# First mixer: the values v made like the gates, from seven half-size products, with half of the weight sums added by transfers

## The chip, the cores and the metric

The kernel runs on one core of one Trainium2 chip. Its time is the device time of one launch in microseconds (us); the median of three runs is given. A profile is one execution recorded by the hardware profiler.

## The reference

The whole trunk has two layers, each a token mixer and a gated ConvFFN, with a LayerNorm after each. The change is in the first mixer, gated linear attention (GLA). Cut to what matters:

```python
def gla_mixer(x, w_in, w_gk2, b_gk, norm_w, w_out):      # x: 512 x 1024
    hk, hv = GLA_HEADS * GLA_DK, GLA_HEADS * GLA_DV      # 512, 1024
    proj = x @ w_in
    q, k, v, gate, gk_lr = jnp.split(proj, [hk, 2 * hk, 2 * hk + hv, 2 * hk + 2 * hv], axis=-1)
    gk = jax.nn.log_sigmoid((gk_lr @ w_gk2 + b_gk).astype(jnp.float32)) / GLA_NORMALIZER
    ...
    o = rms_norm(gla_chunked(qc, kc, vc, gc), norm_w)    # 4 heads, chunks of 64
    o = from_head_chunks(o).astype(x.dtype)
    return (o * jax.nn.silu(gate)) @ w_out
```

So v and the gates are both a product of x (512 x 1024) with a 1024 x 1024 part of w_in: v from column 1024, the gates from column 2048.

## The kernel before, in words

**Precision.** Every large product is made from three: a number is split into a high part in fp32r (ScalarE, a cast) and a low part (VectorE, the number less its high part), and high x high, high x low and low x high are summed in PSUM. `split_out` (line 714) is that pair of operations; its tiles are `wh` and `wl` for weights, `xh` and `xl` for x. `raw` is a loaded block of weights (128 x 1024 floats, 512 KB).

**Weights.** A plan lists the blocks of weights in the order of their use. SyncE loads them ahead into three `raw` buffers; a block is issued (cast and split) up to two or three blocks ahead of TensorE (`LOOKAHEAD`, `self.look`). Four pairs of `wh` and `wl` buffers exist, so a cast waits until TensorE is done with the block four before it; a load waits until the split of the block three before it in `raw`.

**The first mixer in stages.** (1) x is loaded, turned and split; q, k and the low-rank factor are made feature by feature (tiles `fm`). Beside them `prepare(hd)` makes the decays of head hd: a small product `z`, then exponentials on ScalarE and a scan and some ten products on VectorE (tiles `z`, `na`, `bc`, `e`). (2) v is made by `x_tm` (tiles `tm`): two halves of 512 columns, each 4 blocks of weights, each block against 4 groups of 128 tokens. A ScalarE copy takes each result out of PSUM (line 1518). Beside them `scores` makes the scores (`sa`) of two heads and `turn` their turned keys (`kt`). (3) The gates are made by `gated` (tiles `fold`, then `sg`), and beside them `core(hd)` runs the four heads: the products `ds` with v, the states on VectorE, the outputs `o`. `finish` multiplies the outputs with the gates. (4) The output product.

**Seven for eight.** `gated` cuts the 512 tokens, the 1024 inputs and the 1024 outputs in two each, which makes 8 products of quarter matrices; with sums of quarters of x (the forms `w1`, `v2`, `v3`, `v4`, made by `x_forms` on VectorE) and of w, 7 do (`GATED`: b11, b21, t1, t2, b22, t3, t4). Each of the 7 takes two blocks of weights (i = 0 and 2), each block against two groups of 128 tokens (r = 0, 1), with two chunks of inputs (j) in three terms: 2 x 2 x 2 x 3 = 24 matmuls of 128 x 512. They gather in four PSUM tiles, two for each of the two sides (`acc`). What a product adds to the results is taken out by `update`: by ScalarE copies, or by VectorE additions and subtractions of a PSUM tile and a kept tile (lines 1230, 1237, 1240). The sums of w are made on VectorE in `issue_gated`: t1 and t2 add a loaded block to the kept b11 block (`gw`, line 451), t3 subtracts and t4 adds (lines 454 and 456), two blocks each.

**The order of the work.** The program is one thread per engine. The main line pumps matmuls of the stage, and the smaller jobs (`prepare`, `scores`, `core`, `finish`) are tasks that are let in between by a modelled clock; a scheduler then fixes each engine's order. An engine takes its instructions strictly in that order, so an instruction that waits holds all behind it.

**Accumulating transfers** exist already in the ConvFFN's output product (lines 408 and 410): GpSimd issues a DMA that adds its source to a block in SBUF.

Of the kernel before, what the change touches and what calls it, by code (L numbers as in the profile page):

```python
# [12 lines left out]
AF = mybir.ActivationFunctionType  # L13
ALU = mybir.AluOpType

P = 128
# [16 lines left out]
GATED = (("b11", "a11", 0), ("b21", "a12", 1), ("t1", "w1", 1), ("t2", "v2", 0), ("b22", "v4", 1), ("t3", "v3", 0),  # L33
         ("t4", "a22", 0))
GATED_NEW = {"b11": "b11", "b21": "b21", "t1": "b12", "t2": "b22", "b22": "b22", "t3": "b11", "t4": "b21"}
LN_EPS = 1e-5
RMS_EPS = 1e-6
GLA_SCALE = 128.0 ** -0.5
# [30 lines left out]
def blk(i, n=P):  # L69
    return slice(i * n, i * n + n)  # L70


class Trunk:
# [339 lines left out]
    def issue_fold(self, group, name, quarter, i):  # L413
# [11 lines left out]
            self.fold_sum(*following[1:3], following[4])  # L425
        return [(wh[:, blk(j, S)], wl[:, blk(j, S)]) for j in range(n)]

    def gated_load(self, group, name, i):


        if name == "b11":
            t = self.mp.tile([P, 1024], F32, name=self.uid("gw"), tag="gw", bufs=2)
        else:
            t = self.rp.tile([P, 1024], F32, name=self.uid("raw"), tag="raw")
        quarter = GATED_NEW[name]
        col = group["col"] + (2 - int(quarter[2])) * S
        c0 = 2 * i + int(quarter[1]) - 1
        src = group["w"].rearrange("(c p) f -> p c f", p=P)[:, c0:c0 + 3:2, col:col + S]
        load = self.nc.sync.dma_start(t.rearrange("p (j f) -> p j f", j=2), src)
        if name == "b11":  # L440
            self.behind(load, self.load)
        group[name, i] = t

    def issue_gated(self, group, name, i):
        nc = self.nc
        t = group.pop((name, i))
        if name == "b11":
            group["sum", i] = t
        total = group["sum", i]
        if name in ("t1", "t2"):  # L450
            nc.vector.tensor_add(total, total, t)
            t = total
        elif name == "t3":
            nc.vector.tensor_sub(t, total, t)
        elif name == "t4":
            nc.vector.tensor_add(t, total, t)
            del group["sum", i]
        self.vec(1.24)
# [688 lines left out]
    def x_forms(self, forms):  # L1147


        nc = self.nc  # L1150
        pair = lambda t: t.rearrange("p (j i) -> p j i", j=2)

        def part(x, odd, tok, k):
            return x[:, 4 * k + odd:4 * k + odd + 3:2, tok:tok + 256]

        def full(odd, tok):
            ts = [self.slot("xq") for _ in range(2)]
            for k, t in enumerate(ts):
                self.behind(nc.vector.tensor_add(pair(t), *(part(x, odd, tok, k) for x in (self.xh, self.xl))),
                            self.split[1])  # L1160
            return ts

        def split(name, ts):
            forms[name] = []
            for t in ts:
                h, l = self.slot("xfh", F32R), self.slot("xfl", F32R)
                self.split_out(h, l, t)
                forms[name].append((h, l))
            self.set(("form", name), 2.0)

        def both(a, b, op, out):
            for x, y, o in zip(a, b, out):
                nc.vector.tensor_tensor(o, x, y, op)

        a = full(0, 256)
        yield 2.0
        b = full(1, 256)
        yield 2.0
        both(a, b, ALU.subtract, b)
        yield 3.0  # L1180
        split("w1", b)
        yield 3.0
        c = full(0, 0)
        yield 2.0
        both(c, a, ALU.subtract, a)
        yield 2.0
        both(b, c, ALU.subtract, b)
        yield 3.0
        split("v2", b)
        yield 3.0  # L1190
        c = full(1, 0)
        yield 2.0
        both(b, c, ALU.add, b)
        yield 3.0
        split("v4", b)
        b = c = None
        yield 4.0
        split("v3", a)

    def gated(self, sg, forms):  # L1200


        nc = self.nc
# [9 lines left out]
            return self.xh[:, chunk, tok:tok + P], self.xl[:, chunk, tok:tok + P]  # L1213

        def copied(ps):
            t = self.slot("sg")
            nc.scalar.copy(t, ps)
            return t

        def done(tb, hf, t, src):  # L1220
            nc.scalar.activation(t, src, AF.Silu)
            sg[tb][hf] = t
            self.set(("sg", tb, hf), 1.2)

        def update(name, r):
            p, x = acc[0][r], acc[1][r]
            if name == "b11":
                top[r] = copied(p)
            elif name == "b21":
                nc.vector.tensor_add(top[r], top[r], x)  # L1230
                done(r, 1, top[r], top[r])
            elif name == "t1":
                high[r] = copied(x)
            elif name == "t2":
                right[r] = copied(p)
            elif name == "b22":
                nc.vector.tensor_sub(right[r], x, right[r])
                done(r, 0, right[r], right[r])
            elif name == "t3":
                self.third = nc.vector.tensor_sub(high[r], high[r], p)  # L1240
                self.after = None, self.third
                done(2 + r, 0, high[r], high[r])
            elif name == "t4":
                done(2 + r, 1, self.slot("sg"), p)

        self.look = 3
        for name, form, at in GATED:
            if form[0] in "vw":
                self.wait(("form", form))
            for i in (0, 2):  # L1250
                if name == "t3" and i:
                    self.look = 2
                w = self.weight()
                if name == "t4":
                    self.after = ()
                for r in range(2):
# [9 lines left out]
            forms.pop(form, None)  # L1266
        self.look = LOOKAHEAD

    def gates(self, sg):
# [59 lines left out]
    def gla(self, li, g, b):  # L1329
# [10 lines left out]
        def lr_done(ps):  # L1340
# [75 lines left out]
        sg = [[None, None] for _ in range(NTB)]  # L1416
        y = [[None, None] for _ in range(NTB)]

        kts, turned = [None] * GH, []

        def turn(hd):
            pk = self.psum("kt")
# [4 lines left out]
        def scores(first):  # L1427
# [4 lines left out]
            for hd in pair:  # L1432
# [18 lines left out]
        def core(hd):  # L1451
# [59 lines left out]
            self.spawn(scores(hd))  # L1511
        for hd in range(GH):
            self.spawn(core(hd))
        forms = {}
        for hf in range(2):
            def v_done(tb, ps, hf=hf):
                v[tb][hf] = t = self.slot("v")
                nc.scalar.copy(t, ps)
                self.set(("v", tb, hf), 2.4)
# [538 lines left out]
```

## Time and profile before

| | |
|---|---|
| median of three runs | 1226.43 us (1226.0 to 1226.56) |
| the profiled execution | 1226.47 us |
| its span | 1224.8 us, so 1.7 us lie outside it |
| TensorE busy | 1218.5 us, 99% |
| VectorE, ScalarE, GpSimd busy | 897.4, 604.7, 145.5 us |
| moved by transfers | 146.25 MB, 119 GB/s over the span |

In the profile PE is TensorE, PEld its loading of the stationary operand, DVE VectorE, ACT ScalarE, POOL GpSimd, SP SyncE; a q behind a name is that engine's sequencer. A row of a group gives line, engine, operation, out<-in with shapes and count, then busy time and mean ns of one, then the idle time of the engine just before and what ended it. A row of a timeline gives start and duration in us. Stage (1) lasts to about 60 us, v from there to about 90, the gates to about 168.

### The profile page before, as it was taken

The numbers are of one execution on the slowest core, as the hardware profiler recorded it, in microseconds if no ns is written. First come the engines' busy times: TensorE is split into PE (matmuls) and PEld (weight loads), VectorE is DVE, ScalarE is ACT, GpSimd is POOL, SyncE is SP. The second block draws the span as 40 slices with busy tenths as digits, with TensorE's granted clock in tenths as the row PEclk, the third lists the DMA queues.
The fourth block names the chain that finished last, engine by engine and source line by source line (L and its number), as shares of the span: only waits on it lengthen the run. The fifth ranks groups of instructions, "written<-read, shape, count | busy, mean of one in ns | idle before, by whom it ended". The sixth has DMA issues, their size and how long they took to land.

```text
span 1224.8 us, 17199 instructions
## 1 busy us (share of the span) xinstructions
PE 1218.5 (99%) x6525; PEld 1029.5 (84%) x6525; DVE 897.4 (73%) x1507; ACT 604.7 (49%) x1066; POOL 145.5 (12%) x191
## 2 busy tenths in 40 slices
PE   9999999999999999999999999999999999999998
PEld 8888888988888888889888888988988888888886
DVE  4976987686757775766789975688687756775667
ACT  5655764544434443554678555544644434443440
POOL 4000000601100010001252030200520100020000
PEclk9999999999999999999999999999999999999999
DMA  7332353545843454333344341235343763383311
GB/s 210 116 103 70 88 187 96 164 123 122 201 123 103 112 112 120 105 113 95 105 129 130 102 135 36 88 120 155 125 134 94 160 194 90 104 183 88 107 65 69
DMA packets 174642, 146.25 MB, mean 119 GB/s; under 512 B 16774, under 2 KB 140746, under 8 KB 174560
## 3 DMA queue, kind: packets, MB, share of 16 engines
q1 hardware_dynamic: 164096, 119.43, 32.6%
q0 software_dynamic: 9504, 25.08, 9.8%
q8 instruction: 51, 0.84, 0.3%
q10 hardware_dynamic: 960, 0.66, 0.2%
q14 instruction: 31, 0.25, 0.1%
HBM read 126.77 MB, written 5.78 MB: 108 GB/s over the span
## 4 chain that ended last, share of the span: by engine, by line
PE 99%; DVE 0%; ACT 0%; issue 0%; DVEq 0%; POOL 0%; POOLq 0%
PE fm L209 54%; PE tm L209 20%; PE fold L209 16%; PE o L209 2%; PE xT L227 1%; PE pq L209 1%; PE pg L209 1%; PE vn L209 1%; PE yT L227 1%; PE V L209 0%; PE qs L209 0%; PE s L209 0%; PE ks L209 0%; PE ds L209 0%; PE warm L796 0%; PE sa L209 0%
## 5 line engine op out<-in xcount | busy, mean ns | idle before, releaser
L209 PE MATMUL fm<-xh,wh 128*128 128x512 f32 (+2 forms) x1096 | 400.4, 368 | 0.7 <-ACT xh L714 0.7
L209 PE MATMUL fm<-xl,wh 128*128 128x512 f32 (+2 forms) x1096 | 398.5, 366 | 0.0
L209 PE MATMUL fm<-xh,wl 128*128 128x512 f32 (+1 forms) x1072 | 391.4, 367 | 0.0
L714 DVE TENSOR_TENSOR wl<-raw,wh 128x1024 fp32r<-128x1024 f32 (+1 forms) x162 | 200.7, 1241 | 166.6 <-ACT wh L714 166.4
L714 ACT CAST wh<-raw 128x1024 fp32r<-128x1024 f32 (+1 forms) x163 | 169.0, 1038 | 213.8 <-PE fm L209 139.6
L209 PEld LDWEIGHTS fm<-xh,wh 128*128 128x128 f32 (+1 forms) x1096 | 205.4, 188 | 34.1 <-ACT xh L714 0.9
L209 PEld LDWEIGHTS fm<-xl,wh 128*128 128x128 f32 (+1 forms) x1096 | 205.4, 188 | 32.9
L209 PEld LDWEIGHTS fm<-xh,wl 128*128 128x128 f32 x1072 | 201.3, 189 | 33.1
L1017 DVE SCALAR_TENSOR_TENSOR conv<-fm,ffn_cw,conv 128x511 f32<-128x511 f32 x112 | 83.5, 745 | 10.1 <-ACT conv L1015 8.4
L209 PE MATMUL fold<-wh,fh 128*128 128x512 f32 x224 | 87.6, 391 | 0.0
L209 PE MATMUL fold<-wh,fl 128*128 128x512 f32 x224 | 87.2, 389 | 0.0
L209 PE MATMUL fold<-wl,fh 128*128 128x512 f32 x224 | 87.1, 389 | 0.0
L714 ACT CAST wh<-b 128x1024 fp32r<-128x1024 f32 x48 | 50.0, 1054 | 74.2 <-PE fold L209 36.1
L714 DVE TENSOR_TENSOR wl<-b,wh 128x1024 fp32r<-128x1024 f32 x48 | 58.1, 1222 | 22.7 <-ACT wh L714 22.4
L408 POOL DMA_DIRECT2D b<-b x24 | 20.9, 916 | 357.0 <-DVE wl L714 309.8
L1035 ACT ACTIVATE conv<-conv 128x512 f32<-128x512 f32 x44 | 27.8, 632 | 64.3 <-DVE conv L1017 64.3
L1574 DVE SCALAR_TENSOR_TENSOR conv<-fm,gdn_cw,conv 128x511 f32<-128x511 f32 (+2 forms) x72 | 53.9, 787 | 5.1 <-ACT conv L1572 4.6
L927 POOL TENSOR_TENSOR h<-h,gb 128x512 f32<-128x512 f32 x16 | 23.5, 1484 | 256.2 <-PE xT L227 248.4
L209 PE MATMUL tm<-wh,xh 128*128 128x512 f32 x128 | 52.5, 410 | 0.0
L209 PEld LDWEIGHTS fold<-wh,fh 128*128 128x128 f32 x224 | 42.0, 188 | 9.6 <-DVE h L1106 1.0
L209 PE MATMUL tm<-wl,xh 128*128 128x512 f32 x128 | 50.1, 391 | 0.0
L209 PE MATMUL tm<-wh,xl 128*128 128x512 f32 x128 | 50.0, 391 | 0.0
(359 smaller groups left out, 1962.9 us busy)
## 6 DMA issues: line engine op xcount, KB each, us to landing
raw<-in_ffn_w_in_dram SPq DMA_DIRECT2D x88, 512.0 KB, 3.7
raw<-in_gdn_w_in_dram SPq DMA_DIRECT2D x32, 512.0 KB, 4.1
raw<-in_gla_w_in_dram SPq DMA_DIRECT2D x26, 512.0 KB, 3.5
b<-in_ffn_w_out_dram SPq DMA_DIRECT2D x24, 512.0 KB, 6.6
b<-b POOLq DMA_DIRECT2D x24, 512.0 KB, 4.6
raw<-in_ffn_w_out_dram SPq DMA_DIRECT2D x20, 512.0 KB, 3.6
raw<-in_gla_w_out_dram SPq DMA_DIRECT2D x8, 512.0 KB, 3.6
b<-in_ffn_w_out_dram POOLq DMA_DIRECT2D x8, 512.0 KB, 5.7
```

Source lines behind the costliest of these rows:

```text
L209: t = self.nc.tensor.matmul(out, a, b, start=start, stop=stop, skip_group_check=joined)
L227: t = self.nc.tensor.transpose(out, a, self.ident[:n, :n])
L408: self.nc.gpsimd.dma_start(out, group[src, i][:, cols], accum_op=ALU.add)
L714: return self.nc.scalar.copy(dst_h, src), self.nc.vector.tensor_sub(dst_l, src, dst_h)
L927: nc.gpsimd.tensor_mul(h[hf], h[hf], gb[hf])
L1017: nc.vector.scalar_tensor_tensor(a[:, d:], ps[:, :S - d], tap(2 - d), a[:, d:], ALU.mult, ALU.add)
L1035: nc.scalar.activation(a, a, AF.Gelu)
L1574: self.conv = nc.vector.scalar_tensor_tensor(a[:, d:], ps[:, :S - d], tap(3 - d), a[:, d:], ALU.mult, ALU.add)
```

## The change

v is made by `gated` too, with the same forms of x, and `x_tm` is no longer used for it. The forms are made in stage (1), ahead of v, and kept until the gates are done. `PREPARE` spreads the four `prepare` tasks: heads 2 and 3 come later, beside v. The scores of a pair of heads are turned right after they are made. Product b21 now comes before b11.

The sums of w for t3 and t4 move from VectorE to transfers: t3's block is b12, onto which GpSimd adds b22 from DRAM; t4's block is what t2 left in `gw`, onto which GpSimd adds b21 from DRAM once t2's block is split. t1 and t2 stay VectorE additions, for the gates and now for v.

```diff
-GATED_NEW = {"b11": "b11", "b21": "b21", "t1": "b12", "t2": "b22", "b22": "b22", "t3": "b11", "t4": "b21"}
+GATED_NEW = {"b21": "b21", "b11": "b11", "t1": "b12", "t2": "b22", "b22": "b22", "t3": "b12"}
+PREPARE = (4.0, 16.0, 48.0, 72.0)
...
     def gated_load(self, group, name, i):
+        if name == "t4":
+            return
...
-        load = self.nc.sync.dma_start(t.rearrange("p (j f) -> p j f", j=2), src)
-        if name == "b11":
-            self.behind(load, self.load)
+        t3 = t.rearrange("p (j f) -> p j f", j=2)
+        self.nc.sync.dma_start(t3, self.gated_rows(group, GATED_NEW[name], i))
+        if name == "t3":
+            self.nc.gpsimd.dma_start(t3, self.gated_rows(group, "b22", i), accum_op=ALU.add)
         group[name, i] = t
...
     def issue_gated(self, group, name, i):
...
         if name in ("t1", "t2"):
+            total = group["b11", i]
             nc.vector.tensor_add(total, total, t)
             t = total
-        elif name == "t3":
-            nc.vector.tensor_sub(t, total, t)
-        elif name == "t4":
-            nc.vector.tensor_add(t, total, t)
-            del group["sum", i]
...
         self.split_out(wh, wl, t)
         self.vec(1.24)
+        if name == "t2":
+            nc.gpsimd.dma_start(t.rearrange("p (j f) -> p j f", j=2), self.gated_rows(group, "b21", i),
+                                accum_op=ALU.add)
...
-            if name == "b11":
-                top[r] = copied(p)
-            elif name == "b21":
-                nc.vector.tensor_add(top[r], top[r], x)
+            if name == "b21":
+                top[r] = copied(x)
+            elif name == "b11":
+                nc.vector.tensor_add(top[r], top[r], p)
                 done(r, 1, top[r], top[r])
...
-        for hf in range(2):
-            for cp in range(NC // 2):
-                self.plan_tm(w_in, 2 * cp * P, 2, 1024 + hf * S)
+        self.plan_gated(w_in, 1024)
         self.plan_gated(w_in, 2048)
...
-                self.spawn(prepare(hd), 4.0 + 6.0 * hd)
+                self.spawn(prepare(hd), PREPARE[hd])
...
+        forms = {}
+        self.spawn(self.x_forms(forms))
         self.fm_items(items)
...
-            for other in turned:
-                turn(other)
-            turned[:] = pair
+            yield SCORES_APART
+            for hd in pair:
+                turn(hd)
             if first:
-                yield SCORES_APART
-                for hd in pair:
-                    turn(hd)
                 self.turn_columns()
...
-            self.x_tm(v_done)
-            if hf == 0:
-                self.spawn(self.x_forms(forms), 4.0)
+        self.gated(forms, "v", v_done, False)
         for hf in range(2):
             for half in range(2):
                 self.spawn(finish(hf, half))
-        self.gated(sg, forms)
+        self.gated(forms, "sg", gate_done, True)
```

In the changed program the line numbers are some seven higher (714 becomes 721, 1240 becomes 1243; its 1240 is the old 1237, and 1225 is the old 1217).

The order of ScalarE at the end of v, before. `wh` rows are casts of weights, `v<-tm` the copies of v out of PSUM, `o` the outputs of head 0; here stand the four copies of v's second half with their neighbours:

```order
L714 CAST xfh_1147<-xq_1059 128x512
L714 CAST wh_1193<-gw_1108 128x1024
L714 CAST wh_1237<-raw_1161 128x1024
L1518 COPY v_1205<-tm_987 128x512
L1518 COPY v_1215<-tm_988 128x512
L1518 COPY v_1223<-tm_989 128x512
L1518 COPY v_1231<-tm_990 128x512
```

ScalarE after, at the change from t2 to t3 of v. `raw_918` and `raw_949` are t3's two blocks, `gw_661` is t4's first; `e` and `bc` are exponentials of head 2; `v_986` and `v_994` are the copies of t2's two PSUM tiles, into which t3 goes next:

```order
L721 CAST wh_945<-raw_892 128x1024
L721 CAST wh_976<-raw_918 128x1024
L1378 ACTIVATE e_178_942<-e_177_940 128x512
L1379 ACTIVATE e_177_940<-e_177_940 128x512
L721 CAST wh_999<-raw_949 128x1024
L1383 ACTIVATE e_182_964<-e_182_964 128x512
L1389 ACTIVATE e_183_967<-e_183_967 128x512
L1390 ACTIVATE bc_938<-bc_938 128x512
L1225 COPY v_986<-fold_741 128x512
L1225 COPY v_994<-fold_742 128x512
L721 CAST wh_1016<-gw_661 128x1024
```

Before, the copies stand behind casts of blocks that SyncE loaded; after, behind the cast of a block that a transfer of GpSimd completes, and behind three exponentials.

VectorE before, in the gates from b22's joinings to t3's (lines 1237 and 1240; `sg` are gates, `wl` splits, line 1503 products of `finish`):

```order
L1237 TENSOR_TENSOR sg_1538<-fold_1235,sg_1538 128x512
L1237 TENSOR_TENSOR sg_1546<-fold_1236,sg_1546 128x512
L456 TENSOR_TENSOR raw_1553<-gw_1108,raw_1553 128x1024
L1503 SCALAR_TENSOR_TENSOR sg_1538<-o_1011,gla_rr_737,sg_1538 128x256
L1503 SCALAR_TENSOR_TENSOR sg_1538<-o_1048,gla_rr_737,sg_1538 128x256
L1503 SCALAR_TENSOR_TENSOR sg_1546<-o_1011,gla_rr_737,sg_1546 128x256
L714 TENSOR_TENSOR wl_1590<-raw_1553,wh_1589 128x1024
L1503 SCALAR_TENSOR_TENSOR sg_1546<-o_1048,gla_rr_737,sg_1546 128x256
L1240 TENSOR_TENSOR sg_1475<-sg_1475,fold_1233 128x512
L1240 TENSOR_TENSOR sg_1505<-sg_1505,fold_1234 128x512
```

VectorE after, the same place of the product scheme, in v. `wl_1000` is the split of t3's second block, `wl_1017` and `wl_1037` those of t4, `wl_1069` that of the gates' b21; the line-1240 rows join b22, the line-1243 rows join t3; `e_183` and `bc` belong to head 2:

```order
L1398 TENSOR_TENSOR e_183_967<-e_183_967,qk_655 128x4x64
L1399 TENSOR_TENSOR e_183_967<-e_183_967,qk_601 128x4x64
L721 TENSOR_TENSOR wl_1000<-raw_949,wh_999 128x1024
L1401 TENSOR_TENSOR bc_938<-bc_938,qk_601 128x512
L721 TENSOR_TENSOR wl_1017<-gw_661,wh_1016 128x1024
L1240 TENSOR_TENSOR v_986<-fold_743,v_986 128x512
L1240 TENSOR_TENSOR v_994<-fold_744,v_994 128x512
L721 TENSOR_TENSOR wl_1037<-gw_709,wh_1036 128x1024
L721 TENSOR_TENSOR wl_1069<-raw_1020,wh_1068 128x1024
L1243 TENSOR_TENSOR v_927<-v_927,fold_741 128x512
L1243 TENSOR_TENSOR v_935<-v_935,fold_742 128x512
```

The line-456 addition is gone from between the two joinings; two splits now stand directly ahead of the second joining, and operations of a head's preparation stand ahead of the first.

More of the change, by code (lines that the diff above doesn't have):

```diff
@@ L32 @@
 FOLD = [(n, FOLD_NEW[n], *FOLD_ALL[n]) for n in ("b11", "b21", "t1", "t2", "b22", "t3", "t4")]
-GATED = (("b11", "a11", 0), ("b21", "a12", 1), ("t1", "w1", 1), ("t2", "v2", 0), ("b22", "v4", 1), ("t3", "v3", 0),
+GATED = (("b21", "a12", 1), ("b11", "a11", 0), ("t1", "w1", 1), ("t2", "v2", 0), ("b22", "v4", 1), ("t3", "v3", 0),
          ("t4", "a22", 0))
-GATED_NEW = {"b11": "b11", "b21": "b21", "t1": "b12", "t2": "b22", "b22": "b22", "t3": "b11", "t4": "b21"}
+GATED_NEW = {"b21": "b21", "b11": "b11", "t1": "b12", "t2": "b22", "b22": "b22", "t3": "b12"}
+PREPARE = (4.0, 16.0, 48.0, 72.0)
 LN_EPS = 1e-5
@@ L426, in issue_fold, with gated_rows @@
         return [(wh[:, blk(j, S)], wl[:, blk(j, S)]) for j in range(n)]
+    def gated_rows(self, group, quarter, i):
+        col = group["col"] + (2 - int(quarter[2])) * S
+        c0 = 2 * i + int(quarter[1]) - 1
+        return group["w"].rearrange("(c p) f -> p c f", p=P)[:, c0:c0 + 3:2, col:col + S]
     def gated_load(self, group, name, i):
+        if name == "t4":
+            return
         if name == "b11":
@@ L434, in gated_load @@
             t = self.rp.tile([P, 1024], F32, name=self.uid("raw"), tag="raw")
[L435 to L438, printed above, removed]
-        load = self.nc.sync.dma_start(t.rearrange("p (j f) -> p j f", j=2), src)
-        if name == "b11":
-            self.behind(load, self.load)
+        t3 = t.rearrange("p (j f) -> p j f", j=2)
+        self.nc.sync.dma_start(t3, self.gated_rows(group, GATED_NEW[name], i))
+        if name == "t3":
+            self.nc.gpsimd.dma_start(t3, self.gated_rows(group, "b22", i), accum_op=ALU.add)
         group[name, i] = t
@@ L445, in issue_gated @@
         nc = self.nc
-        t = group.pop((name, i))
-        if name == "b11":
-            group["sum", i] = t
-        total = group["sum", i]
+        if name == "t4":
+            t = group.pop(("b11", i))
+        elif name == "b11":
+            t = group[name, i]
+        else:
+            t = group.pop((name, i))
         if name in ("t1", "t2"):
+            total = group["b11", i]
             nc.vector.tensor_add(total, total, t)
             t = total
-        elif name == "t3":
-            nc.vector.tensor_sub(t, total, t)
-        elif name == "t4":
-            nc.vector.tensor_add(t, total, t)
-            del group["sum", i]
-        self.vec(1.24)
+            self.vec(1.24)
         self.held += 1
@@ L1158, in full @@
             for k, t in enumerate(ts):
-                self.behind(nc.vector.tensor_add(pair(t), *(part(x, odd, tok, k) for x in (self.xh, self.xl))),
-                            self.split[1])
+                nc.vector.tensor_add(pair(t), *(part(x, odd, tok, k) for x in (self.xh, self.xl)))
             return ts
@@ L1173, in both, with gated @@
                 nc.vector.tensor_tensor(o, x, y, op)
+        for tb in range(NTB):
+            yield from self.until(("x", tb))
         a = full(0, 256)
-        yield 2.0
-        b = full(1, 256)
-        yield 2.0
[L1179 to L1190, printed above, removed]
+        yield 1.5
+        b = full(1, 256)
+        yield 1.5
+        both(a, b, ALU.subtract, b)
+        yield 1.5
+        split("w1", b)
+        yield 2.0
+        c = full(0, 0)
+        yield 1.5
+        both(c, a, ALU.subtract, a)
+        yield 1.5
+        both(b, c, ALU.subtract, b)
+        yield 1.5
+        split("v2", b)
+        yield 2.0
         c = full(1, 0)
-        yield 2.0
+        yield 1.5
         both(b, c, ALU.add, b)
-        yield 3.0
+        yield 1.5
         split("v4", b)
         b = c = None
-        yield 4.0
+        yield 2.0
         split("v3", a)
-    def gated(self, sg, forms):
+    def gated(self, forms, tag, done, last):
         nc = self.nc
@@ L1215, in copied @@
         def copied(ps):
-            t = self.slot("sg")
+            t = self.slot(tag)
             nc.scalar.copy(t, ps)
             return t
[L1220 to L1223, printed above, removed]
         def update(name, r):
             p, x = acc[0][r], acc[1][r]
-            if name == "b11":
-                top[r] = copied(p)
-            elif name == "b21":
-                nc.vector.tensor_add(top[r], top[r], x)
+            if name == "b21":
+                top[r] = copied(x)
+            elif name == "b11":
+                nc.vector.tensor_add(top[r], top[r], p)
                 done(r, 1, top[r], top[r])
@@ L1243, in update @@
             elif name == "t4":
-                done(2 + r, 1, self.slot("sg"), p)
+                done(2 + r, 1, self.slot(tag), p)
         self.look = 3
@@ L1265, in gated @@
                 self.spend()
-            forms.pop(form, None)
+            if last:
+                forms.pop(form, None)
         self.look = LOOKAHEAD
@@ L1417, in gla @@
         y = [[None, None] for _ in range(NTB)]
-        kts, turned = [None] * GH, []
+        kts = [None] * GH
         def turn(hd):
@@ L1513, in gla, with v_done, gate_done @@
             self.spawn(core(hd))
[L1514 to L1519, printed above, removed]
-            self.x_tm(v_done)
-            if hf == 0:
-                self.spawn(self.x_forms(forms), 4.0)
+        def v_done(tb, hf, t, src):
+            if src is not t:
+                nc.scalar.copy(t, src)
+            v[tb][hf] = t
+            self.set(("v", tb, hf), 1.2)
+        def gate_done(tb, hf, t, src):
+            nc.scalar.activation(t, src, AF.Silu)
+            sg[tb][hf] = t
+            self.set(("sg", tb, hf), 1.2)
+        self.gated(forms, "v", v_done, False)
         for hf in range(2):
```

## The prediction

> **What bounds the kernel now.** I read the page first, then the waits of TensorE, then the chain in order of time around the stage that makes v. The page gives the span, each engine's busy share and the chain that ended last:
>
> ```profile
> span 1224.8 us, 17199 instructions
> PE 1218.5 (99%) x6525; PEld 1029.5 (84%) x6525; DVE 897.4 (73%) x1507; ACT 604.7 (49%) x1066; POOL 145.5 (12%) x191
> PEclk9999999999999999999999999999999999999999
> PE 99%; DVE 0%; ACT 0%; issue 0%; DVEq 0%; POOL 0%; POOLq 0%
> ```
>
> TensorE is the chain, at its full granted clock in every slice. A busy TensorE can still be a slow one, so I look for its idle time; this is the whole answer for its waits:
>
> ```profile
> PE warm L796 <- POOL one L98: 1.0, 1, 1.0
> PE fm L209 <- ACT xh L714: 0.7, 1, 0.7
> PE mid L209 <- ACT diag L943: 0.6, 1, 0.6
> ```
>
> 2.3 us in all, none of it in the first mixer after 8 us. So a matmul taken out shortens the kernel by its own pitch, as long as the other engines keep up with a TensorE that arrives earlier. The pitch comes from the chain from 54 to 100 us (start, duration, what, number of matmuls):
>
> ```profile
> 59.72 5.44 PE tm L209 x24
> 65.16 2.01 PE sa L209 x48
> ...
> 79.98 0.87 PE kt L227 x8
> ...
> 90.79 1.29 PE ds L209 x6
> ```
>
> 24 wide matmuls take 5.44 us, 0.227 each. (The groups show 390 ns for one; that duration overlaps the next.) The v stage begins at 59.72.
>
> **The change, part by part.** *Matmuls.* The groups of the first 260 us show one term of v as it is now, and the two kinds of product of the gates, which already have the new form:
>
> ```profile
> L209 PE MATMUL tm<-wh,xh 128*128 128x512 f32 x64 | 25.8, 403 | 0.0
> L209 PE MATMUL fold<-wh,xfl 128*128 128x512 f32 x32 | 12.6, 393 | 0.0
> L209 PE MATMUL fold<-wh,xh 128*128 128x512 f32 x24 | 10.1, 422 | 0.0
> ```
>
> v takes 3 terms of 64, the new form 3 of 32 + 24 = 56: 3 x 8 = 24 matmuls fewer, 24 x 0.227 = 5.44 us off the chain. This is the only gain; the DVE additions taken out of the gates are off the path, as TensorE waits for nothing there.
>
> *What VectorE and ScalarE get.* The stretch from the end of the first weights to the last gates, 20 to 168 us (PE, PEld, DVE, ACT, POOL busy), and groups of DVE and ACT in it:
>
> ```profile
> 20.00:168.00 148.00, 148.00 (x799) 125.30 (x798) 117.22 (x229) 90.63 (x158) 1.65 (x4) 1.00 0.34 103
> L714 DVE TENSOR_TENSOR wl<-raw,wh 128x1024 fp32r<-128x1024 f32 x24 | 29.2, 1219 | 16.6 <-ACT wh L714 16.5
> L451 DVE TENSOR_TENSOR gw<-gw,raw 128x1024 f32<-128x1024 f32 x4 | 4.9, 1220 | 0.0
> L1471 DVE COPY state<-ds 128x256 f32<-128x256 f32 x4 | 1.7, 422 | 5.7 <-PE ds L209 5.7
> L1240 DVE TENSOR_TENSOR sg<-sg,fold 128x512 f32<-128x512 f32 x2 | 1.3, 678 | 0.0
> L714 ACT CAST wh<-gw x6: 1046/1048/1055, 99.2 to 138.2; 128x1024 fp32r<-128x1024 f32 x6
> L1518 ACT COPY v<-tm x4: 587/587/587, 84.0 to 88.1; 128x512 f32<-128x512 f32 x4
> ```
>
> v's weights become 14 splits instead of 8: 6 x 1.22 = 7.3 us of DVE, 6 x 1.05 = 6.3 of ACT. Its t1 and t2 need 4 additions (4.9) and the joining of products 6 PSUM operations (6 x 0.68 = 4.1). The gates lose the 4 operations of L454 and L456 (-4.9). DVE: 117.2 + 11.4 = 128.6 us, to be done in 148.0 - 5.4 = 142.6. It is 90% full where it was 79%. The forms of x (16 operations and 8 splits) and two heads' preparation move within this stretch and cost nothing in the sum. ACT goes to 97 of 142.6 and is no bound.
>
> *The transfers.* In the v stage SyncE brings 12 blocks and GpSimd adds 4 more into them; before, SyncE brought 8. The two b11 blocks are loaded in the first microseconds, 1 MB ahead of the second block of q and k weights. The transfer engines' share of two stretches there (before the last number), and when that second block is cast now:
>
> ```profile
> 8.00:12.00 4.00, 4.00 (x37) 4.00 (x36) 3.51 (x6) 2.73 (x5) 0.25 (x1) 1.00 1.15 317
> ...
> 20.00:24.00 4.00, 4.00 (x36) 4.00 (x35) 0.68 (x1) 1.16 (x2) 1.65 (x4) 1.00 0.42 107
> ```
>
> ```profile
> 23.46 1.05 ACT L714 CAST wh<-raw 128x1024 fp32r<-128x1024 f32 x1 [2.08 <-PE fm L209]
> ```
>
> The queues are full to about 20 us; 1.05 MB at 317 GB/s make that 23.3, and the second block, first of those behind, lands well before its cast at 23.46, which waits for TensorE and not for a transfer. I cost it at nothing, and at up to 1 us if the blocks behind slip. What the accumulating transfers cost is to be bounded from the ones that add ffn_w_out, from DRAM and from SBUF (line 410's, then line 408's, least, median and most; the POOL instruction; an ordinary block):
>
> ```profile
> L410 POOL DMA_DIRECT2D b<-in_ffn_w_out_dram x8: 1202/1205/1224, 317.5 to 1097.6; - x8
> DMA to landing us min/median/max: 5.5/5.7/7.5
> ...
> DMA to landing us min/median/max: 4.5/4.6/8.7
> raw<-in_gla_w_in_dram SPq DMA_DIRECT2D x26, 512.0 KB, 3.5
> ```
>
> I take 5.7, the row of the same kind (source in DRAM, 512 KB); the ends are 4.5 and 8.7. [...]
>
> *First wait: t3 of v.* Without waits TensorE gets there at 59.26 (59.72 less two z products of 0.23, which now come later) + 5 products of 24 x 0.227 = 27.2 + sa 2.01 + kt 0.87 + one z 0.23 = 89.6. t3 writes the bank that t2 filled, so it waits for the ScalarE copy of t2. That copy stands behind the cast of t3's second block (the ACT rows above), and the cast behind that block's accumulating transfer. The block's buffer comes free with the split of b22's first block. The weight buffer of that cast comes free halfway through t1, at 75.7 (59.26 + 2 products of 5.44, sa, kt and half of t1, 2.7); cast 1.05 and split 1.22 bring 78.0. Then the load, 3.5: 81.5, the accumulation, 5.7: 87.2, the cast, 1.05: 88.25. ScalarE then does three exponentials of head 2. Their pitch, and that of DVE's operations, from the timelines of before (start, duration):
>
> ```profile
> 60.83 0.62 ACT L1387 ACTIVATE e<-e 128x512 f32<-128x512 f32 x1
> 61.35 0.62 ACT L1388 ACTIVATE bc<-bc 128x512 f32<-128x512 f32 x1
> ```
>
> ```profile
> 154.28 1.23 DVE L714 TENSOR_TENSOR wl<-raw,wh 128x1024 fp32r<-128x1024 f32 x1 [0.49 <-ACT wh L714]
> 155.43 1.28 DVE L1237 TENSOR_TENSOR sg<-fold,sg 128x512 f32<-128x512 f32 x2
> 156.62 1.22 DVE L456 TENSOR_TENSOR raw<-gw,raw 128x1024 f32<-128x1024 f32 x1
> ```
>
> 0.52 apart, the last 0.62: 89.9; the copy, 0.59: 90.5. TensorE waits 0.9 us. With a transfer of 4.5 it waits nothing, of 7.5 2.7.
>
> *Second wait: t4 of v.* t4 starts in the bank that t3's first half filled, and VectorE must have subtracted it from v first. Nominally t4 comes at 89.6 + 5.44 + 4 of ds's matmuls (0.86) = 95.9. The subtraction is the tenth row of the DVE excerpt above, behind two splits of t4, one of the gates' b21, t3's own and b22's two joinings. The queue is held by the exponential that ended at 89.9: then a 128x4 copy and two half-wide products of head 2 (0.8), split 1.15, product 0.6, split 1.15, two joinings 1.2, two splits 2.3, the subtraction 0.68: 97.8. That is 1.9 after 95.9, and 0.9 of it has been waited already; 1.0 is added. Before, in the gates, the one split and one product stand there, and the subtraction ran at 160.63 beneath transposes:
>
> ```profile
> 161.00 0.87 PE yT L227 x8
> 161.88 4.13 PE fold L209 x18
> ```
>
> In v no transposes are there. Followed in the same way through the order to the end of the gates, no instruction of TensorE's is later than these waits have made it. So the two together cost 1.9, bounded by 0.7 (a transfer of 4.5) and by 3.7 (7.5) or 4.9 (8.7).
>
> *Sum.* The profiled execution took 1226.47 us (span 1224.8 and 1.7 around it), the median 1226.43; no difference that matters. 1226.47 - 5.44 + 1.9 = 1222.9.
>
> **The rivals.** *All covered.* If the transfers take 4.6 or less and VectorE gets through its rows 0.8 us sooner than I count, the 5.44 us come whole: 1221.0. For it: line 408's median, and that rows of one engine overlap by some 0.08 each, which I counted only in part. Against: the source is DRAM, as in line 410, and by the order of GpSimd's queue three accumulations (the first block of t3, the first of t4, the second of t3) stand close behind each other.
>
> *Slow accumulations.* If they lengthen each other, as the rows' 7.5 and 8.7 show can happen, the cost is 3.7 to 4.9: 1224.7 to 1225.9, no difference to be told. A measurement of this kernel can tell about 0.2%, 2.45 us, from no change. For it: the overlap just named. Against: half of line 410's stayed between 5.5 and 5.7. [...]
>
> *VectorE becomes the bound.* TensorE's gain needs VectorE's idle time in the stretch to fall from 30.8 (148.0 - 117.2) to 14.0. Its waits for casts (16.6) and for ds (5.7) stay if they are chains (TensorE frees a buffer, ScalarE casts, VectorE splits): 128.6 + 22.3 = 150.9 instead of 148.0, 2.9 slower: 1229.4. The place is the end of v and the start of the gates, where heads 2 and 3 are now prepared between splits. It decides once more than 19.4 us of idle time stay. Against: buffers let a cast run ahead by two blocks, and most of those waits are slack of an engine that had nothing due.
>
> *The change doesn't do what it says.* 24 matmuls fewer are in the program's order; so this has no chance of its own; only the transfers and the queues are open.
>
> **How the numbers follow.** Forecast (waits of 0.7 to 3 us) 0.46, 1222.9; all covered 0.20, 1221.0; slow accumulations 0.20, 1224.7 to 1225.9; VectorE bound 0.14, 1229.4. Faster by over 0.2% means below 1223.98: the first two less 0.04 of the first's upper end, 0.62. Within: 0.20 + 0.04 = 0.24. Slower (above 1228.88): 0.14. The range runs from all covered, 1221.0, less the 0.3 by which runs differ (1226.0 to 1226.56), to the slow end, 1225.9, with the early loads' 1 us on it: 1220.7 to 1226.9. It leaves out the VectorE case and little else.
>
> **What would show it.** Right: 168 wide matmuls in v; TensorE's waits list a fold matmul waiting for ACT's copy of v near 90 us and one for DVE near 97, 1 us each; the accumulating transfers on GpSimd's queue land in 5.7 us; from the gates on every start is 3.5 us earlier. Wrong: no wait there (all covered), landings above 7 us, waits spread over ten or more matmuls of the gates for DVE's splits (VectorE the bound), or a wait before 30 us (the early loads).

## The result, and the profile after

The changed kernel takes 1234.99 us (median of 6 runs, 1234.4 to 1236.14), the one before 1226.49 beside it: ratio 1.007, 95% interval 1.0057 to 1.0083. It is 8.5 us slower, where 3.5 us faster was forecast, and it lies outside the range. The profiled execution's span is 1232.9 us against 1224.8, so 8.1 us more are to be found.

The page of the changed kernel shows the matmuls gone and TensorE's share of the chain down; in the clock line the fourth of the 40 slices, 92 to 123 us, has fallen below nine tenths:

```profile
span 1232.9 us, 17199 instructions
PE 1217.2 (99%) x6501; PEld 1027.6 (83%) x6501; DVE 912.1 (74%) x1519; ACT 609.2 (49%) x1072; POOL 155.6 (13%) x199
PEclk9998999999999999999999999999999999999999
q0 software_dynamic: 11680, 29.28, 12.0%
PE 94%; DMA 2%; DVE 2%; ACT 1%; issue 0%; DVEq 0%; POOL 0%; ACTq 0%; POOLq 0%
```

6501 matmuls against 6525: 24 fewer, as the sum had it. TensorE's waits after (total, times, longest); the last three are those of before:

```profile
PE fold L210 <- ACT v L1225: 7.4, 1, 7.4
PE yT L228 <- DVE sg L1504: 2.2, 1, 2.2
PE warm L803 <- POOL one L99: 1.0, 1, 1.0
PE fm L210 <- ACT xh L721: 0.7, 1, 0.7
PE mid L210 <- ACT diag L950: 0.6, 1, 0.6
```

The first is the predicted first wait, at the predicted matmul, for the predicted copy: 7.4 us instead of 0.9. The second wait forecast is not there as a wait of its own; another stands in the gates. The chain of the changed kernel around the first (start, duration, what), which can be laid beside the prediction's steps one by one:

```profile
75.66 1.06 ACT wh L721
...
76.74 1.24 DVE wl L721
...
77.99 7.65 DMA raw<-in_gla_w_in_dram
...
86.21 7.36 DMA raw<-in_gla_w_in_dram
...
94.60 0.62 ACT e L1383
95.22 0.52 ACT e L1389
95.74 0.52 ACT bc L1390
96.26 0.48 ACT v L1225
...
96.78 7.69 PE fold L210 x24
```

Cast 75.66 (forecast 75.7), split done at 78.0 (78.0): right to a tenth. Then the load takes 7.65 us instead of 3.5 and the accumulating transfer 7.36 instead of 5.7 (with 0.6 between them), and TensorE starts at 96.78 instead of 90.5. The last row has a second loss in it: 24 matmuls in 7.69 us, where 5.44 was the pitch. The timeline of TensorE shows why:

```profile
89.04 0.39 PE L210 MATMUL fold<-wh,xfl 128*128 128x512 f32 x1
96.78 0.79 PE L210 MATMUL fold<-wh,xfh 128*128 128x512 f32 x1 [7.36 <-ACT v L1225]
97.38 0.63 PE L210 MATMUL fold<-wl,xfh 128*128 128x512 f32 x1
97.80 0.63 PE L210 MATMUL fold<-wh,xfl 128*128 128x512 f32 x1
...
100.79 0.46 PE L210 MATMUL fold<-wh,xfh 128*128 128x512 f32 x1
101.09 0.40 PE L210 MATMUL fold<-wl,xfh 128*128 128x512 f32 x1
```

After the wait a matmul starts every 0.43 us, for 4.0 us, and then every 0.23 again: the granted clock was halved. The windows give it as a number (clock, share of the transfer engines and GB/s are the last three):

```profile
82.00:84.00 2.00, 2.00 (x10) 1.67 (x9) 2.00 (x3) 0.24 (x1) 0.00 (x0) 1.00 1.03 272
90.00:92.00 2.00, 0.00 (x0) 0.00 (x0) 0.00 (x0) 0.00 (x0) 0.00 (x0) 1.00 1.08 191
94.00:98.00 4.00, 1.22 (x3) 1.02 (x4) 2.40 (x5) 4.00 (x7) 0.00 (x0) 0.51 0.00 0
...
158.40:176.20 17.80, 17.80 (x83) 14.89 (x84) 16.13 (x28) 11.71 (x20) 0.00 (x0) 0.90 0.19 60
```

The account: 24 matmuls fewer -5.44; the wait at t3 of v +7.4 and the slow clock behind it +2.25 (7.69 - 5.44); the wait before the gates' turned outputs (yT) +2.2 and the slow clock behind that +1.8 (17.8 x 0.10). Sum +8.2, measured +8.1; a part may be off by some tenths.

### The profile page after: what moved, and what is told of

It reads as the page before. It is cut to its first block, busy times and chain, and to the rows that moved or that the text cites. A ratio compares the mean times of both kernels' runs of the same rounds, so it can differ in the third digit from the quotient of the medians.

```text
span 1232.9 us, 17199 instructions
## 1 busy us (share of the span) xinstructions
PE 1217.2 (99%) x6501; PEld 1027.6 (83%) x6501; DVE 912.1 (74%) x1519; ACT 609.2 (49%) x1072; POOL 155.6 (13%) x199
## 4 chain that ended last, share of the span: by engine, by line
PE 94%; DMA 2%; DVE 2%; ACT 1%; issue 0%; DVEq 0%; POOL 0%; ACTq 0%; POOLq 0%
PE fm L210 54%; PE tm L210 16%; PE fold L210 16%; DMA raw<-in_gla_w_in_dram 2%; PE xT L228 1%; PE o L210 1%; DVE wl L721 1%; PE pq L210 1%; PE pg L210 1%; PE vn L210 1%; PE yT L228 1%; PE V L210 0%; PE qs L210 0%; PE s L210 0%; PE ks L210 0%
## 5 line engine op out<-in xcount | busy, mean ns | idle before, releaser
L721 DVE TENSOR_TENSOR wl<-raw,wh 128x1024 fp32r<-128x1024 f32 (+1 forms) x158 | 196.3, 1245 | 154.5 <-ACT wh L721 154.4
L721 ACT CAST wh<-raw 128x1024 fp32r<-128x1024 f32 (+1 forms) x159 | 164.6, 1037 | 219.7 <-PE fm L210 132.9
L210 PE MATMUL fold<-wh,fl 128*128 128x512 f32 x224 | 87.2, 389 | 0.0
L210 PEld LDWEIGHTS fold<-wh,fl 128*128 128x128 f32 x224 | 42.1, 188 | 8.8
L210 PEld LDWEIGHTS fold<-wl,fh 128*128 128x128 f32 x224 | 42.1, 188 | 8.6
L1024 DVE SCALAR_TENSOR_TENSOR form<-fm,ffn_cw,form 128x511 f32<-128x511 f32 x64 | 47.7, 746 | 1.1
L721 ACT CAST fh<-form 128x1792 fp32r<-128x1792 f32 (+3 forms) x24 | 28.7, 1194 | 24.4 <-DVE form L1065 12.9
```

The costliest lines, as they stand in the source:

```text
L210: t = self.nc.tensor.matmul(out, a, b, start=start, stop=stop, skip_group_check=joined)
L721: return self.nc.scalar.copy(dst_h, src), self.nc.vector.tensor_sub(dst_l, src, dst_h)
L1024: nc.vector.scalar_tensor_tensor(a[:, d:], ps[:, :S - d], tap(2 - d), a[:, d:], ALU.mult, ALU.add)
```

## The experiments

Three theories of the waits were set against each other. A: the transfers are late because the accumulating ones crowd the transfer engines. B: VectorE's added work is the bound (the slower rival of the prediction). C: an accumulating transfer is slow by itself, whatever runs beside it, and (as the later experiments put it) costs the chain wherever it stands. All kernels but the last (e13) do v by seven products.

**All sums on VectorE (e1).** t3's and t4's blocks are loaded plain and joined by `tensor_sub` and `tensor_add`, in v and in the gates:

```diff
-        if name == "t3":
-            self.nc.gpsimd.dma_start(t3, self.gated_rows(group, "b22", i), accum_op=ALU.add)
+        elif name == "t3":
+            nc.vector.tensor_sub(t, group["b11", i], t)
+        elif name == "t4":
+            nc.vector.tensor_add(t, group.pop(("b11", i)), t)
```

> v from seven products as in the change, but all sums of weights on VectorE, in v and in the gates: no accumulating transfer in the mixer. Theory A (the two waits come from transfers that are late because the accumulating ones crowd the transfer engines, and TensorE's clock falls after the long wait): both waits and the slow clock go, 1221 to 1224 us. Theory B (VectorE's added work is the bound): VectorE has 8 x 1.22 = 9.8 us more to do than in the changed kernel, so as slow or slower, 1235 or more. Theory C (an accumulating transfer of such a block is slow by itself, crowding or not): 1221 to 1224, as by A.

Measured 1224.27 us (1223.88 to 1225.0; ratio to before 0.9981, 0.9972 to 0.9991). B fell: with eight additions more on VectorE (8 x 1.22 = 9.8 us of them; its busy time grows from 912.1 to 918.5 us) the kernel is 10.7 us faster than the changed one. The time is 0.3 above the range of A and C, between which this run can't choose. Its waits:

```profile
PE fold L212 <- DVE wl L732: 1.3, 1, 1.3
PE fold L212 <- DVE v L1254: 0.5, 1, 0.5
PE yT L230 <- DVE sg L1515: 0.4, 1, 0.4
```

What VectorE costs as a full engine is this: 2.2 us in three places, not a shift of the whole stretch.

**One kind of transfer at a time (e2, e3).** e2 has t3's sum on VectorE and t4's by transfer, e3 the reverse.

> t3's sum on VectorE, t4's by an accumulating transfer that is issued when t3 is split; v and gates. Theory A: half of the accumulating transfers and none on the way to t3, so the wait at t3 of v goes: 1221 to 1225 us. Theory B: VectorE has 4.9 us more than in the changed kernel, 1235 or more. Theory C: t4's transfer takes 7 us instead of 5.7, and comes late for t4: 1223 to 1227.

Measured 1224.88 us (ratio 0.9986, 0.9977 to 0.9996), within the ranges of A and of C.

> t3's sum by an accumulating transfer as in the change, t4's on VectorE; v and gates. Theory A: with t4's accumulating transfers gone the load and the accumulation of t3's second block take 4 and 5.7 us instead of 7.65 and 7.36, the wait falls from 7.4 to 1 to 3 us: 1222 to 1226 us. Theory B: 1235 or more. Theory C: the accumulation still takes over 7 us, the wait is 4 us or more and the clock falls: 1227 to 1232.

Measured 1233.26 us (1231.83 to 1233.96; ratio 1.0054, 1.0039 to 1.0069), with these waits:

```profile
PE fold L212 <- ACT v L1236: 6.4, 1, 6.4
PE yT L230 <- DVE sg L1515: 1.5, 1, 1.5
```

So the damage is done by t3's transfers, and A as I had put it, with t4's transfers as the crowd, missed: without them the wait is still 6.4 us. C's three signs are there (an accumulation of over 7 us, a wait of over 4, a lower clock: 0.60 from 94 to 98 us), though the time is 1.3 us above its range. In e3 the accumulation of the late block was issued at 84.77 and its cast began at 92.93: 8.1 us, beside two plain loads for t4. That such a transfer isn't that slow by itself is read from the changed kernel, from t4's four (least, median, most):

```profile
DMA to landing us min/median/max: 5.7/6.9/9.5
```

The 5.7 is the first of the gates, issued at 134.03, while the engines were less loaded (0.74 of their time from 134.0 to 139.8 us, against 0.94 in v from 74 to 94); it is the median of line 410's. The 9.5 was issued at 77.42, amid two more accumulating transfers and a plain load. So in company the transfers took longer here (the four in v 6.5 to 9.5 us, with the engines busy for 0.85 to 1.09 of the time), and in e3 plain loads were company enough.

**t4's transfers later (e7).** The edit was meant to issue them when t3 is split.

> As the changed kernel, but t4's accumulating transfers are issued when t3 is split instead of when t2 is; v and gates. All eight remain. Theory A: the load of t3's second block has the transfer engines to itself and one accumulation, so the wait at t3 falls to 1 to 3 us; t4's transfers come later and one may be late for t4: 1223 to 1228 us. Theory B: unchanged, 1234 to 1236. Theory C: t3's wait 4 us or more, 1228 to 1234.

Measured 1234.92 us. It told nothing: the scheduler put the transfers where they had been (GpSimd's timeline has t4's first at 74.14, in the changed kernel 73.93). It is a second measurement of the changed kernel.

**The late block loaded early (e8, e9).** The transfers stay, but t3's second block (e8) or both blocks (e9) have buffers of their own, so that their loads no longer wait for one of the three `raw` buffers. Two buffers cost four of the mixer's 47 slots. The orders of TensorE, VectorE and ScalarE are those of the changed kernel.

```diff
+        elif name == "t3" and i:          # e9: elif name == "t3"
+            t = self.mp.tile([P, 1024], F32, name=self.uid("tw"), tag="tw", bufs=1)
```

> The changed kernel, but the second block of t3 has a buffer of its own (in v and in the gates), so that SyncE loads it and GpSimd adds to it long before it is cast; the orders of TensorE, VectorE and ScalarE stay as in the changed kernel. All eight accumulating transfers remain. Theory A (late because it is loaded late into engines that are crowded): the wait of 7.4 us at t3 of v and the slow clock behind it go, the wait at the gates' turned outputs too; what remains is the predicted wait of VectorE before t4: 1221 to 1225 us. Theory C (an accumulating transfer costs the chain wherever it stands): 1228 or more. Theory B fell with the sums on VectorE and would have 1233 or more here.

> As the run before, but both blocks of t3 have buffers of their own. Theory A: like the run before or up to 1 us less, as the first block's accumulation no longer falls beside other loads: 1221 to 1224 us. Theory C: 1228 or more.

Measured e8 1226.38 us (1224.55 to 1228.47; ratio 0.9998, 0.999 to 1.0007), e9 1225.74 (1223.85 to 1226.85; 0.9991, 0.9982 to 1.0). What C says of the chain fell: all eight transfers are there, no shorter than before (t3's in e9 6.5 to 9.1 us to landing), and 8.6 to 9.3 us are gone, because hardly anybody waits for them. Both times lie above A's ranges all the same. In e8 the wait in the gates, which was to go, stayed:

```profile
PE yT L228 <- DVE sg L1506: 2.4, 1, 2.4
```

Its chain goes back to the transfer of t3's first block (issued at 136.74, landed 8.46 us later), which in e8 still lies in `raw`; in e9 this wait is gone and another has come (last section). e8's TensorE in v waits at the two places that the prediction named, once the late block is out of the way:

```profile
90.88 0.50 PE L210 MATMUL fold<-wh,xfh 128*128 128x512 f32 x1 [1.15 <-ACT v L1227]
98.80 0.47 PE L210 MATMUL fold<-wh,xh 128*128 128x512 f32 x1 [1.31 <-DVE v L1245]
```

1.15 us at t3 for ScalarE's copies, 1.31 at t4 for VectorE's joining; 0.9 and 1.0 were forecast. That the sizes agree is luck: what holds ScalarE's queue here is the cast of t3's first block, at 85.60, which waited for an accumulating transfer of 8.15 us. e9 has only 0.3 us there, and yet is no faster than e1; see the last section.

**One stage at a time (e5, e6).** e5 has accumulating transfers in the gates only, e6 in v only.

> Weight sums of v on VectorE, those of the gates by accumulating transfers as in the change. Theory A: v as with all sums on VectorE (waits of about 2 us in sum), the gates as in the changed kernel (a wait of 2.2 us before the turned outputs and about 1.7 us of slow clock): 1226 to 1229 us. If the gates' wait is only an echo of v's (all was 6 us later by then): 1223 to 1225.

> The reverse: v's sums by accumulating transfers, the gates' on VectorE. Theory A: v's wait of 7.4 us and 2.2 us of slow clock stay, the gates' go: 1230 to 1232 us.

Measured e5 1227.74 us (ratio 1.001, 1.0001 to 1.0019) and e6 1231.94 (1.0047, 1.0032 to 1.0062), both as A had them. The wait before yT is 2.6 us in e5 and 0.4 in e6:

```profile
PE yT L230 <- DVE sg L1515: 2.6, 1, 2.6
PE yT L230 <- DVE sg L1515: 0.4, 1, 0.4
```

It belongs to the gates' own transfers and is no echo of v's. There ScalarE's cast of t3's first block (in the changed kernel its transfer was issued at 142.93 and landed at 151.18) holds up the copies and squares of a head's outputs, on which the last gates' products wait.

**The cast behind the copies (e10).** The transfers stay late; only ScalarE's order changes, so that the copies no longer stand behind the cast that waits:

```diff
-        self.split_out(wh, wl, t)
+        cast, _ = self.split_out(wh, wl, t)
+        if name == "t3":
+            self.behind(cast, self.freed)      # the last copy of t2
```

> The changed kernel, with one ordering rule more: ScalarE's cast of t3's second block goes behind the copies of t2 and the exponentials, in v and in the gates. The transfers stay as late as they are. If the wait of 7.4 us is made by the queue of ScalarE (the copies stand behind a cast that waits for a transfer landing at 93.6): TensorE does t3's first block (2.7 us) meanwhile and waits for the second block's high part at about 94.7 and its low part at about 95.9, 3.6 us in sum instead of 7.4: 1228.5 to 1231.5 us. If TensorE needed the late block itself for its first matmul of t3: unchanged, 1234 to 1236.

Measured 1230.24 us (1228.07 to 1231.6). TensorE does t3's first block and waits for the second:

```profile
91.92 0.39 PE L210 MATMUL fold<-wh,xfl 128*128 128x512 f32 x1
94.99 0.80 PE L210 MATMUL fold<-wh,xfh 128*128 128x512 f32 x1 [2.68 <-ACT wh L723]
96.25 0.80 PE L210 MATMUL fold<-wl,xfh 128*128 128x512 f32 x1 [0.46 <-DVE wl L723]
```

By the medians, 4.75 us of the loss were thus not the late transfer but what stood behind it in ScalarE's queue. The size is rough: e10's runs lie 3.5 us apart, and those with the lowest granted clock (0.995 and 0.996, as in the changed kernel) took 1231.5 and 1231.6, 3.5 less than the changed one. The cast itself began at 93.89, in the changed kernel at 93.65.

**A better kernel (e11, e12).** e11 is e1 with heads 2 and 3 prepared later, so that the sums come ahead of head 2's products on VectorE; e12 has early-loaded transfers in v and VectorE's sums in the gates.

```diff
-PREPARE = (4.0, 16.0, 48.0, 72.0)
+PREPARE = (4.0, 16.0, 60.0, 80.0)
```

> All sums of weights on VectorE (as in the first experiment), and the preparation of heads 2 and 3 spawned later (60 and 80 instead of 48 and 72), so that VectorE does t3's and t4's sums ahead of head 2's products. Theory A with VectorE's queue as what is left: the waits of 1.3, 0.5 and 0.4 us of the first experiment shrink: 1222 to 1224 us. If the later preparation comes late for the scores and heads in the gates: 1225 to 1229.

> Accumulating transfers in v only, t3's blocks of v in buffers of their own and so loaded early; the gates' sums on VectorE. Theory A: v nearly without a wait (0.3 us, as with both blocks in own buffers), the gates with 0.4: 1221.5 to 1224 us.

Measured e11 1223.96 us (1223.08 to 1224.69; ratio 0.9979, 0.997 to 0.9987), e12 1225.13 (0.9988, 0.9979 to 0.9997), 1.1 above its range for a wait at the mixer's end (last section). e11 is the fastest kernel here, 2.5 us under the one before; one wait of 1.5 us for VectorE's joining before t4 is left in v. e1 and e11 are not told apart with certainty.

**The moved work alone (e13).** v by eight full products as before, everything else as in e1.

> What the change moves, without what it is about: v by eight full products as before, the gates' sums on VectorE, but the forms of x made early, heads 2 and 3 prepared later and the scores turned at once, as in the change. The moves cost nothing by the prediction: 1226 to 1227 us. If they cost the microsecond that the first experiment's waits leave unexplained: 1227 to 1228.

Measured 1227.18 us (ratio 1.0005, 0.9996 to 1.0014): no wait of TensorE is added. The median is 0.7 us above before; the interval leaves room for anything from nothing to 1.7 us. The 24 matmuls are then worth 1227.18 - 1224.27 = 2.9 us in e1, net of its waits.

## Why the prediction was wrong

*The matmuls: right.* 24 fewer; e1, e8 and e11 show the gain when the waits are taken off. e1's span is 2.0 us under before: -5.44 and 2.4 of waits make -3.0. The rest, 1.0, may be what a stop costs beyond its listed wait: the last matmul before it counts as busy for 0.39 us although the next could have started after 0.23, and the first behind it takes longer (0.50). Four stops at about 0.2 are 0.8, an estimate; what the moved work costs (e13) is not told apart from it.

*The places of the waits in v: right.* The copy of t2 behind the cast, the cast behind the transfer (e10 shows the queue), the joining before t4 (e8; in the changed kernel the long first wait covers it). That the forms, heads and early loads cost nothing: right as far as e13 can tell (no new wait before 30 us in the changed kernel, and 0.2 and 0.4 us for a block of x in e1 and e8).

*The step that failed* is "Then the load, 3.5: 81.5, the accumulation, 5.7: 87.2". I took a median of transfers (5.7), half of which landed in 5.5 to 5.6 us while the engines were busy for 0.67 to 0.72 of the time, as the price of each of several that run at once, and bounded it by the most that one such row had shown. The load measured 7.65, the accumulation 7.36: of the 6.3 us by which TensorE came later than forecast, 4.15 are the plain load, 1.66 the accumulation and 0.6 the time from the load's landing to GpSimd's issue. The load grew with the accumulating transfers that were under way when it was issued, none in e5 (at 78.46), one in e3 (78.23), three in the changed kernel (77.99):

```profile
DMA to landing us min/median/max: 3.7/3.7/3.7
DMA to landing us min/median/max: 5.9/5.9/5.9
DMA to landing us min/median/max: 7.7/7.7/7.7
```

What would have told is the time that the transfers need of the engines together, which the queue rows hold. Before, for 119.43 MB of plain transfers and for 25.08 MB from GpSimd's queue:

```profile
q1 hardware_dynamic: 164096, 119.43, 32.6%
q0 software_dynamic: 9504, 25.08, 9.8%
```

A plain block (0.524 MB) takes 0.326 x 1224.8 x 0.524 / 119.43 = 1.75 us of all 16 engines. GpSimd's queue grew from 0.098 x 1224.8 = 120.0 us to 0.12 x 1232.9 = 147.9 with the 8 new transfers: 3.5 us each, twice a plain block. That needed the changed kernel, but a stretch around one of line 410's transfers gives nearly as much before: 0.67 x 5.6 = 3.8 us for 110 GB/s x 5.6 us = 0.62 MB. It stands here ahead of the crowded window of the changed kernel (share of the transfer engines next to last):

```profile
447.20:452.80 5.60, 5.60 (x27) 4.62 (x26) 5.59 (x8) 2.46 (x3) 1.20 (x1) 1.00 0.67 110
```

```profile
74.00:94.00 20.00, 15.43 (x68) 12.41 (x67) 11.24 (x15) 7.39 (x11) 4.75 (x4) 1.00 0.94 208
```

208 GB/s for 20 us are 4.16 MB, or eight blocks: four accumulating transfers (14 us) and four plain loads (7) make 21 us of engine time by these prices; 0.94 x 20 = 18.8 were used, so the prices are a tenth high. From the split that frees the late block's buffer (78.0) to t3 (89.6 by the forecast) there are 11.6 us, and the late block's own load and accumulation are among the last of this queue. The rival "slow accumulations" named the lengthening, but for the accumulating transfers alone and from the same rows (4.9 at most), with nothing on the plain load, the larger part, and no slow clock in it; the rival that would be slower, VectorE, was the wrong one.

*Terms that were missing*: the clock (2.25 and 1.8 us), and the gates. I followed the order through the gates with the same transfer times and found no wait; there it is 2.2 us.

## What to carry to other kernels

Price a transfer by what all transfers of that stretch take of the engines together, and count an accumulating one double, as here (3.5 us against 1.75); a landing time read where the engines were less busy (5.5 to 5.6 us at 0.67 to 0.72 of the time) is the lower end, not the middle (6.5 to 9.5 in v of the changed kernel). Look for what stands behind a cast that waits for a transfer, on its own engine: here 4.75 of the 10.7 us, or 3.5 at equal clock, went by putting that cast behind the copies. And allow for the slow clock on top of a long wait of TensorE: in the changed kernel it cost 2.25 us behind the wait of 7.4 and 1.8 behind that of 2.2, while behind waits of 1.5 us and less the clock stayed.

## What the runs showed of the hardware

*The clock after a wait.* It fell after waits of 6.4 to 7.4 us (the changed kernel, e3, e6, e7), and of 2.7 and 2.3 (e10), 2.6 (e5), 2.4 (e9), 2.2 (the changed kernel) and 2.1 (e7), to half speed (0.50; a matmul of 128x512 every 0.43 us instead of 0.23) for some 3 us (e9, 217.1 to 220.1) to 6 (e10, 95.0 to 101.1, a second wait of 0.46 us among them); behind the wait of 7.4 it was 4.0, behind that of 2.2 it was 3.8. After 1.5 us and less it stayed (e1, e2, e3, e11: a matmul every 0.23 us again), but also after 2.36 (e8, with a clock of 1.00 from 154 to 164 us, behind the wait that ended at 152.3) and 2.3 (e12, whose profiled execution has a mean clock of 1.000). Between 2.1 and 2.4 us the length of a wait alone does not decide in these runs; what else does, none of them shows.

*GpSimd beside VectorE.* In e9's profile TensorE waits 2.4 us at the mixer's end, for the last LayerNorm. VectorE's operations on one column take over a microsecond there, while GpSimd multiplies four tiles:

```profile
211.76 4.98 POOL L936 TENSOR_TENSOR h<-h,gb 128x512 f32<-128x512 f32 x4 [80.75 <-DMA gb<-in_ln_g_dram]
```

```profile
211.03 0.21 DVE L875 BATCH_NORM_AGGREGATE ln_mv<-ln_st 128x2 f32<-128x12 f32 x1
211.28 0.15 DVE L879 TENSOR_SCALAR ln_var<-ln_mv 128x1 f32<-128x1 f32 x1
211.60 0.16 DVE L883 RECIPROCAL ln_rs<-ln_root 128x1 f32<-128x1 f32 x1 [0.17 <-ACT ln_root L877]
211.80 1.25 DVE L884 SCALAR_TENSOR_TENSOR ln_t<-ln_rs,ln_var 128x1 f32<-128x1 f32 x1
213.09 1.22 DVE L885 SCALAR_TENSOR_TENSOR ln_rs<-ln_t,ln_rs 128x1 f32<-128x1 f32 x1
214.34 1.20 DVE L897 SCALAR_TENSOR_TENSOR ln_nb<-ln_mv,ln_rs 128x1 f32<-128x1 f32 x1
```

Each of the three long ones ends within 0.1 us of the end of one of GpSimd's products (4.98 / 4 = 1.25 us each); elsewhere in this trace the same operations take 0.15 to 0.22. That GpSimd held them up is my reading of these rows. In the changed kernel GpSimd makes three such products from 216.68 to 221.10 us, and two subtractions of VectorE there (`xl`, 128x512, at 216.97 and 219.99) take 1.54 and 1.67 us instead of 0.69, while a row of statistics between them (at 218.44) takes 0.68 as elsewhere. e12's profile has the same wait as e9's (2.3 us, on line 910), e8's and e1's have not. GpSimd begins these products at 211.8 us in e9, when the scales land and amid the last LayerNorm, but in e8 at 218.1 and in e1 at 202.7 and 206.3, each time released by TensorE's transposes (xT). e9 and e12 have four slots fewer than e1, e8 two; that this is what moves the scales' loads was not tried.

The spread of runs also grew: 3.9 us in e8, 3.5 in e10, 3.0 in e9 and e12 and 2.6 in e5, against 1.1 in e1. In e9 it goes with the clock: its five runs with a granted clock of 1.000 took 1223.9 to 1224.9 us, as e1 does, and its six with 0.998 or 0.999 took 1225.7 to 1226.9. In its profile the clock stands at 0.50 for 2 us behind the wait of 2.4 us and at 0.67 for 2 more, which costs 1.7 us. In e12 the granted clock is 0.999 or 1.000 in every run, so there the spread has another cause, which stays open.
